# Softmax times values, bound by transfers: the load of the values moved to the end of a pass, and three small edits that go with it

## The chip, the cores and the metric

The kernel runs on one core of one Trainium2 chip. The metric is the device time of one execution, in microseconds (us). Executions of one kernel agree within about 0.15%. The time over the kernel before is always taken against its runs of the same rounds on the same chip. The 95% interval of such a ratio is 0.13 to 0.18% (1.4 to 1.9 us) to either side, so smaller differences between times settle nothing by themselves; each kernel has one trace. In lines of the profile, PE and PEld are TensorE's products and weight loads, DVE is VectorE, ACT ScalarE, POOL GpSimd, SP SyncE; a q marks an engine's sequencer, and L255 is line 255 of the kernel.

## The reference

```python
def reference(scores, v):          # scores (8, 12, 1024, 1024), v (8, 12, 1024, 64), float32
    scores_max = np.max(scores, axis=-1, keepdims=True)
    attn = np.exp(scores - scores_max)
    attn = attn / (np.sum(attn, axis=-1, keepdims=True) + 1e-8)
    return np.matmul(attn, v).astype(np.float32)
```

There are 96 heads. The scores are 403 MB, the values 25 MB, and 25 MB are written. The profile counts 436 MB read.

## The kernel before

One pass of the loop does four heads. A head's scores (4 MB) lie in one of four buffers. ScalarE takes the exp of two rows a partition at a time, TensorE transposes, VectorE copies, TensorE multiplies by the values and a column of ones, VectorE divides. The values of four heads come in one load of 1 MB; GpSimd casts them to 16 bits; VectorE spreads them. Outputs of two heads leave in one store of 128 rows of 4,096 bytes. SyncE issues every transfer, in program order, into one queue. The parts that matter:

```python
    def load_next(k, n0):                       # heads 0 and 1 of the next pass
        if k < AHEAD - 2:
            load(k, (n0 + (AHEAD + k)) % BH, cond=n0 < BH - AHEAD)

    def last(n0):                               # the end of a pass
        before = queued[-1:]
        with tc.If(n0 < BH - 2 * AHEAD) as cmp:             # an ordinary pass (22 of 24)
            queued[:] = before
            load(AHEAD - 2, (n0 + (2 * AHEAD - 2)) % BH)    # "third load"
            load_v((n0 + 2 * AHEAD) % BH)                   # the values
            load(AHEAD - 1, (n0 + (2 * AHEAD - 1)) % BH)    # "fourth load"
            store(n0, AHEAD - T)                            # "second store"
        with cmp.Else():
            with tc.If(n0 < BH - AHEAD) as cmp2:            # the penultimate pass
                queued[:] = before
                load(AHEAD - 2, BH - 2, (4, 4))
                load(AHEAD - 1, BH - 1, (4,))
                store(n0, AHEAD - T)
                load(AHEAD - 1, BH - 1, (2, 1, 1), 4)
            with cmp2.Else():                               # the last pass
                queued[:] = before
                store(n0, AHEAD - T)

    def heads(n0):
        for k in range(AHEAD):
            ...                                 # exp, transposes, copies, products
        while pending:
            finish(pending.pop(0))
        cast_v()
        last(n0)
```

The first store of a pass (heads 0 and 1) is issued while head 2 is worked on, ahead of the third load. So the queue of an ordinary pass is: load 0, load 1, first store, third load, values, fourth load, second store.

The softmax here doesn't subtract the row's maximum and nothing guards it: scores larger than these inputs give would overflow.

Of the kernel before, what the change touches and what calls it, by code (L numbers as in the profile page):

```python
# [8 lines left out]
FP32 = mybir.dt.float32  # L9
FP16 = mybir.dt.float16  # L10
EXP = mybir.ActivationFunctionType.Exp
# [3 lines left out]
def kernel(  # L15
# [6 lines left out]
    nc = tc.nc  # L22
    P = 128
# [4 lines left out]
    BH = B * H  # L28
# [7 lines left out]
    AHEAD = 4  # L36
# [11 lines left out]
    v_bh = v.rearrange("b h (i t) d -> (b h i) (t d)", i=Q)  # L48
# [6 lines left out]
    sb_pool = ctx.enter_context(tc.tile_pool(name="sbpool", bufs=1))  # L55
# [4 lines left out]
    order16 = const_pool.tile([P, P], FP16, name="order16")  # L60

    nc.vector.tensor_copy(  # L62
        out=order16[:].rearrange("p (t j) -> p t j", t=T),
        in_=ident32[:].rearrange("p (j t) -> p t j", t=T),
# [11 lines left out]
    def buffers(pool, count, shape, dtype, name):  # L76
        return [pool.tile(shape, dtype, name=f"{name}{k}") for k in range(count)]

    s_bufs = buffers(sb_pool, AHEAD, [P, R, SK], FP32, "s_nat")
    v_sb = sb_pool.tile([P, C // L, S, L, D], FP32, name="v_sb")  # L80
    v_half = sb_pool.tile([P, C // L, S, L, D], FP16, name="v_half")
    p_bufs = buffers(sb_pool, 8, [P, EB, SK], FP16, "p_nat")
    pt_bufs = buffers(sb_pool, 4, [P, SK], FP16, "pt")
    out_bufs = buffers(sb_pool, 2, [P, T, R, D], FP32, "out_sb")
# [8 lines left out]
    def take(bufs):  # L93
        k = turn.get(id(bufs), 0)
        turn[id(bufs)] = k + 1
        return bufs[k % len(bufs)]
# [4 lines left out]
    def after(a, b):  # L101

        tc.add_manual_dep(
            a.ins,
            b.ins.name,
            mybir.DependencyInfo(mybir.DependencyClass.NoSync, mybir.DependencyReason.DATA),
            reason="order",
        )

    def queue(dma):  # L110

        if queued:
            after(dma, queued[-1])
        queued.append(dma)

    def one(bh, n):
        return bh[bass.ds(n, 1)].rearrange("o p r d -> (o p) r d")

    def normalise(k, st, first, last):

        psO = psO_whole if k % 2 == 0 else psO_banks[first]
        psO = psO[:, :, 0 : G * M].rearrange("p b (g m) -> p b g m", m=M)
        recip = st["recip"][:, first:last]
        nc.vector.reciprocal(out=recip, in_=psO[:, :, :, D : D + 1])  # L124
        h = k % T
        for t in range(T):
            part = slice(t * W, (t + 1) * W)
            rows = st["out_sb"][h * W : (h + 1) * W, t, first * G : last * G, :]
            nc.vector.tensor_tensor(  # L129
                out=rows.rearrange("j (b g) d -> j b g d", g=G),  # L130
                in0=psO[part, :, :, 0:D],
                in1=recip[part].to_broadcast([W, last - first, G, D]),
                op=mybir.AluOpType.mult,
            )

    def finish(u):

        n0, k, r, pt, st = u
        b, g = r // G, r % G
        if r == 0:  # L140
            st["recip"] = take(rc_bufs)
            st["out_sb"] = out_bufs[k // T]
        bank = psO_whole[:, b] if k % 2 == 0 else psO_banks[b][:, 0]
        for c in range(C):
            nc.tensor.matmul(  # L145
                out=bank[:, g * M : (g + 1) * M],
                lhsT=pt[:, c * P : (c + 1) * P],
                rhs=st["vones"][:, c, 0:M],
                start=(c == 0),
                stop=(c == C - 1),  # L150
            )
        if k % 2 == 1:
            if g == G - 1:
                normalise(k, st, b, b + 1)
        elif r == R - 1:
            normalise(k, st, 0, R // G)
        if r == R - 1 and k == T - 1:
            store(n0, 0)

    def store(n0, k):  # L160

        rows = out_bh.rearrange("(m x) y -> m x y", x=P)
        dma = nc.sync.dma_start(
            out=rows[bass.ds((n0 + k) // T, 1)].rearrange("o x y -> (o x) y"),
            in_=out_bufs[k // T][:].rearrange("x t r d -> x (t r d)"),
        )
        for other in stores:
            apart(dma, other)
            apart(other, dma)
        apart(dma, dma)  # L170
        stores.append(dma)
        queue(dma)
# [3 lines left out]
    def apart(dma, other):  # L176
        tc.declare_no_dep(
            dma.ins, other.ins, across_iterations=True, reason="stores of two heads are disjoint"
        )

    def load(k, n, parts=(R,), r=0, **cond):
        for rows in parts:
            queue(
                nc.sync.dma_start(  # L184
                    out=s_bufs[k][:, r : r + rows, :],
                    in_=one(sc_bh, n)[:, r : r + rows, :],
                    **cond,
                )
            )
            r += rows  # L190

    def load_v(n):

        rows = v_bh.rearrange("(m x) y -> m x y", x=P)
        queue(
            nc.sync.dma_start(  # L196
                out=v_sb[:].rearrange("x h s l d -> x (h s l d)"),
                in_=rows[bass.ds(n // AHEAD, 1)].rearrange("o x y -> (o x) y"),
            )
        )  # L200

    def cast_v():
        nc.gpsimd.tensor_copy(out=v_half[:], in_=v_sb[:])  # L203

    def spread_v(k, s, behind=None):

        copy = nc.vector.tensor_copy(  # L207
            out=vones_bufs[k][s * Q : (s + 1) * Q, :, 0:D].rearrange(
                "i (h l) d -> i h l d", l=L
            ),  # L210
            in_=v_half[k * Q : (k + 1) * Q, :, s],
        )
        if behind is not None:
            after(copy, behind)

    def load_next(k, n0):

        if k < AHEAD - 2:
            load(k, (n0 + (AHEAD + k)) % BH, cond=n0 < BH - AHEAD)

    def last(n0):


        before = queued[-1:]

        with tc.If(n0 < BH - 2 * AHEAD) as cmp:  # L226
            queued[:] = before
            load(AHEAD - 2, (n0 + (2 * AHEAD - 2)) % BH)
            load_v((n0 + 2 * AHEAD) % BH)
            load(AHEAD - 1, (n0 + (2 * AHEAD - 1)) % BH)  # L230
            store(n0, AHEAD - T)
        with cmp.Else():
            with tc.If(n0 < BH - AHEAD) as cmp2:
                queued[:] = before
                load(AHEAD - 2, BH - 2, (4, 4))
                load(AHEAD - 1, BH - 1, (4,))
                store(n0, AHEAD - T)
                load(AHEAD - 1, BH - 1, (2, 1, 1), 4)
            with cmp2.Else():
                queued[:] = before  # L240
                store(n0, AHEAD - T)

    def heads(n0):

        for k in range(AHEAD):
            if k == 0:
                for s in range(S):
                    spread_v(k, s)
            st = dict(vones=vones_bufs[k])
            for r in range(R):  # L250
                if r % EB == 0:
                    p_nat = take(p_bufs)
                    rows = 1 if k == AHEAD - 1 and r == R - EB else EB
                    for g in range(0, EB, rows):
                        nc.scalar.activation(  # L255
                            out=p_nat[:, g : g + rows, :].rearrange(
                                "p r (x v) -> p x r v", v=Q * L
                            ),
                            in_=s_bufs[k][:, r + g : r + g + rows, :].rearrange(
                                "p r (i x l) -> p x (r i) l", i=Q, l=L  # L260
                            ),
                            func=EXP,
                        )
                p_row = p_nat[:, r % EB, :].rearrange("p (h q l) -> p h l q", q=P, l=L)
                psT = take(psT_bufs)
                for c in range(C):
                    nc.tensor.transpose(  # L267
                        out=psT[:, c * P : (c + 1) * P],
                        in_=p_row[:, c // L, c % L, :],
                        identity=order16[:],  # L270
                    )
                pt = take(pt_bufs)
                copy = nc.vector.tensor_copy(out=pt[:], in_=psT[:])  # L273
                if k < AHEAD - 1 and r % (R // S) == 0:
                    spread_v(k + 1, r // (R // S), copy)
                if r == R - 1:
                    load_next(k, n0)
                pending.append((n0, k, r, pt, st))
                if len(pending) > LAG:
                    finish(pending.pop(0))  # L280
        while pending:
            finish(pending.pop(0))
        cast_v()
        last(n0)

    assert BH % AHEAD == 0 and BH >= 2 * AHEAD and SK == Q * S * C
# [38 lines left out]
```

## Time and profile before

| | kernel before |
|---|---|
| time, median of the first 3 runs | 1065.68 us (1065.58 to 1066.06) |
| span of the profiled run | 1064.0 us |
| DMA queue | 453.00 MB, 99.2% of the time of 16 engines |
| busiest compute engine | DVE, 74% |
| one pass in the middle | 43.68 us |
| start of the last head's exps to the end | 18.0 us |

The pass is a fifth of the windows of five passes that the prediction shows. What bounds the kernel is read there too.

A landing in the trace is sixteen records, one for each DMA engine ("ring" below). In the kernel before, twelve rings land a score load within about 0.6 us of each other, three land 2 to 2.5 us after the median of these twelve, a lag that they get in the first 70 us and keep, and one ring, at first among the twelve, drifts: its lag over the fast rings grows from 0.4 us (at 69 us) to 2.3 us (at 1030 us).

### The profile page before, as it was taken

How to read it: one execution, taken by the hardware profiler on the slowest of the kernel's cores; microseconds unless marked ns; L12 is line 12 of the kernel's file. 1: busy time of each engine (PE TensorE's matmuls, PEld its weight loads, DVE VectorE, ACT ScalarE, POOL GpSimd, SP SyncE). 2: the span in 40 equal slices, each digit the busy share in tenths (PEclk: the TensorE clock that was granted, in tenths of full speed). 3: DMA queues.
4: the chain of work that ended last, by engine and by line, in shares of the span. 5: the costliest groups of instructions: out<-in, count | busy, mean ns of one | idle time of the engine just before them, and what ended most of it. 6: DMA issues, size and time to landing. Idle time of an engine off the chain costs nothing.

```text
span 1064.0 us, 32161 instructions
## 1 busy us (share of the span) xinstructions
PE 731.4 (69%) x12288; PEld 678.4 (64%) x12288; DVE 786.6 (74%) x1589; ACT 735.6 (69%) x432; POOL 48.1 (5%) x31
## 2 busy tenths in 40 slices
PE   2766766767766677677686776867666777666676
PEld 2665756667666667666575665767565666666675
DVE  3776876868768777677786776868768687687777
ACT  3766776666767668586676866667766668676685
POOL 0000000000000000000000000000000000000000
PEclk9888888878889888888988888888889788898989
DMA  9999999999999999999999999999999999999995
GB/s 397 431 418 434 426 433 434 433 434 432 432 434 432 425 443 430 429 431 428 433 431 436 432 434 434 431 434 424 441 427 434 432 426 435 432 432 428 440 425 236
DMA packets 24772, 453.06 MB, mean 426 GB/s; under 512 B 2752, under 2 KB 2752, under 8 KB 9152
## 3 DMA queue, kind: packets, MB, share of 16 engines
q1 hardware_dynamic: 24768, 453.00, 99.2%
q8 instruction: 4, 0.07, 0.0%
HBM read 436.21 MB, written 25.17 MB: 434 GB/s over the span
## 4 chain that ended last, share of the span: by engine, by line
DMA 81%; ACT 12%; issue 3%; ACTq 1%; PE 1%; DVE 0%; SPq 0%; PEld 0%; DVEq 0%
DMA s_nat<-in_scores_dram 81%; ACT p_nat L255 12%; PE psT L267 1%; ACTq L255 1%; ACTq L226 0%; ACTq L292 0%; PE psO L145 0%; DVE pt L273 0%; PE psO_whole L145 0%; SPq L184 0%; PEld L267 0%; ACTq L320 0%; DVE out_sb L129 0%; SPq L196 0%; PEld L145 0%
## 5 line engine op out<-in xcount | busy, mean ns | idle before, releaser
L255 ACT ACTIVATE p_nat<-s_nat 128x2048 f16<-128x2048 f32 (+1 forms) x408 | 704.8, 1799 | 228.1 <-DMA s_nat<-in_scores_dram 202.2
L267 PE MATMUL psT<-order,p_nat 128*128 128x128 f16 x6144 | 574.9, 246 | 269.9 <-ACT p_nat L255 263.9
L273 DVE COPY pt<-psT 128x1024 f16<-128x1024 f16 x768 | 515.8, 687 | 200.6 <-PE L267 109.4
L267 PEld LDWEIGHTS <-p_nat 128*128 128x128 f16 x6144 | 446.5, 123 | 298.3 <-ACT p_nat L255 295.7
L145 PEld LDWEIGHTS <-pt 128*128 128x128 f16 x6144 | 302.9, 107 | 81.0 <-DVE pt L273 77.7
L145 PE MATMUL psO<-vones,pt 128*128 128x65 f16 x3072 | 177.4, 201 | 53.9 <-DVE pt L273 50.2
L145 PE MATMUL psO_whole<-vones,pt 128*128 128x65 f16 x3072 | 189.9, 211 | 2.7 <-DVE pt L273 2.4
L207 DVE COPY vones<-v_half 32x512 f16<-32x512 f16 x384 | 109.4, 285 | 22.8 <-POOL v_half L203 6.0
L255 ACT ACT_TABLE_LOAD x24 | 30.8, 1283 | 89.8 <-DMA s_nat<-in_scores_dram 81.7
L203 POOL CAST v_half<-v_sb 128x2048 f16<-128x2048 f32 x25 | 47.4, 1896 | 1002.3 <-DVE vones L207 957.1
L129 DVE TENSOR_TENSOR out_sb<-psO,recip 64x256 f32<-64x256 f32 x192 | 81.1, 423 | 6.1
L129 DVE TENSOR_TENSOR out_sb<-psO_whole,recip 64x512 f32<-64x512 f32 x96 | 66.1, 688 | 3.0
L124 DVE RECIPROCAL recip<-psO 128x4 f32<-128x4 f32 x96 | 17.1, 178 | 34.4 <-PE psO L145 17.6
L124 DVE RECIPROCAL recip<-psO_whole 128x8 f32<-128x8 f32 x48 | 9.7, 203 | 4.5 <-PE psT L267 3.9
L71 DVE MEMSET vones<- 128x16 f16 x4 | 0.2, 72 | 0.8 <-PEq L309 0.8
L62 DVE CAST order<-ident 128x128 f16<-128x128 f32 x1 | 0.2, 227 | 0.4 <-POOL ident masks.py:199 0.4
masks.py:199 POOL TENSOR_SCALAR_AFFINE_SELECT ident<-ident 128x128 f32<-128x128 f32 x1 | 0.3, 295 | 0.1
masks.py:197 POOL MEMSET ident<- 128x128 f32 x1 | 0.2, 205 | 0.3 <-POOLq L309 0.3
L309 POOL MEMSET const-float32-0.0<- 128x1 f32 x1 | 0.1, 100 | 0.2 <-issue 0.2
L309 POOL MEMSET const-bfloat16-1.0<- 128x1 bf16 x1 | 0.1, 103 | 0.0
L309 POOL MEMSET const-uint8-127<- 128x1 uint8 x1 | 0.1, 103 | 0.0
L309 POOL MEMSET const-float32-1.0<- 128x1 f32 x1 | 0.1, 100 | 0.0
## 6 DMA issues: line engine op xcount, KB each, us to landing
s_nat<-in_scores_dram SPq DMA_DIRECT2D x96, 4096.0 KB, 35.8
v_sb<-in_v_dram SPq DMA_DIRECT2D x24, 1024.0 KB, 33.1
out_dram<-out_sb SPq DMA_DIRECT2D x48, 512.0 KB, 26.9
s_nat<-in_scores_dram SPq DMA_DIRECT2D x3, 2048.0 KB, 32.4
s_nat<-in_scores_dram SPq DMA_DIRECT2D x1, 1024.0 KB, 25.4
s_nat<-in_scores_dram SPq DMA_DIRECT2D x2, 512.0 KB
```

The source lines that it names most:

```text
L62: nc.vector.tensor_copy(out=order16[:].rearrange("p (t j) -> p t j", t=T), in_=ident32[:].rearrange("p (j t) -> p t j", t=T),)
L71: nc.vector.memset(vo[:, :, D : D + 2], 1.0)
L124: nc.vector.reciprocal(out=recip, in_=psO[:, :, :, D : D + 1])
L129: nc.vector.tensor_tensor(out=rows.rearrange("j (b g) d -> j b g d", g=G), in0=psO[part, :, :, 0:D], in1=recip[part].to_broadcast([W, last ...
L145: nc.tensor.matmul(out=bank[:, g * M : (g + 1) * M], lhsT=pt[:, c * P : (c + 1) * P], rhs=st["vones"][:, c, 0:M], start=(c == 0), stop=(c ...
L203: nc.gpsimd.tensor_copy(out=v_half[:], in_=v_sb[:])
L207: copy = nc.vector.tensor_copy(out=vones_bufs[k][s * Q : (s + 1) * Q, :, 0:D].rearrange("i (h l) d -> i h l d", l=L), in_=v_half[k * Q : ( ...
L255: nc.scalar.activation(out=p_nat[:, g : g + rows, :].rearrange("p r (x v) -> p x r v", v=Q * L), in_=s_bufs[k][:, r + g : r + g + rows, :] ...
L267: nc.tensor.transpose(out=psT[:, c * P : (c + 1) * P], in_=p_row[:, c // L, c % L, :], identity=order16[:],)
L273: copy = nc.vector.tensor_copy(out=pt[:], in_=psT[:])
L309: nc = _bacc.Bacc("TRN2", target_bir_lowering=False, num_devices=1)
```

## The change

Its intent: the values are not needed early, so they go behind the pass's last store, and the fourth score load comes up 1 MB of queue earlier. A transfer of 16 rows of 4 bytes fills the place of the values, so that both branches hand out the same completion semaphores to the loads that follow. A one-column exp at the head of the body makes ScalarE load its table there rather than after the wait for head 0's scores. The cast is written ahead of the last head.

```diff
     v_half = sb_pool.tile([P, C // L, S, L, D], FP16, name="v_half")
+    spare = sb_pool.tile([P, 1], FP16, name="spare")
+    short = sb_pool.tile([16, 1], FP32, name="short")
 ...
+    def align():
+        queue(nc.sync.dma_start(out=short[:], in_=v_bh[0:16, 0:1]))
 ...
             load(AHEAD - 2, (n0 + (2 * AHEAD - 2)) % BH)
-            load_v((n0 + 2 * AHEAD) % BH)
+            align()
             load(AHEAD - 1, (n0 + (2 * AHEAD - 1)) % BH)
             store(n0, AHEAD - T)
+            load_v((n0 + 2 * AHEAD) % BH)
 ...
                 store(n0, AHEAD - T)
+                align()
                 load(AHEAD - 1, BH - 1, (2, 1, 1), 4)
 ...
+        table = nc.scalar.activation(out=spare[:], in_=order16[:, 0:1], func=EXP)
         for k in range(AHEAD):
 ...
-                        nc.scalar.activation(
+                        exp = nc.scalar.activation(
 ...
+                        if k == r == g == 0:
+                            after(exp, table)
 ...
+            if k == AHEAD - 2:
+                cast_v()
         while pending:
             finish(pending.pop(0))
-        cast_v()
         last(n0)
```

## The prediction

> **What bounds the kernel now.** I read the page first: shares, slices, the chain, bytes.
>
> ```profile
> q1 hardware_dynamic: 24768, 453.00, 99.2%
> HBM read 436.21 MB, written 25.17 MB: 434 GB/s over the span
> ...
> DMA s_nat<-in_scores_dram 81%; ACT p_nat L255 12%; PE psT L267 1%; ACTq L255 1%; ACTq L226 0%; ACTq L292 0%; PE psO L145 0%; DVE pt L273 0%; PE psO_whole L145 0%; SPq L184 0%; PEld L267 0%; ACTq L320 0%; DVE out_sb L129 0%; SPq L196 0%; PEld L145 0%
> ```
>
> One queue's packets fill 99.2% of the time of sixteen DMA engines, while no compute engine is busy more than 74% (DVE). The chain is a score load, the exp that frees its buffer, the next load: this alone could be a latency loop (four buffers), which earlier exps would shorten. So I asked whether the transfer engines ever rest, with sums over windows of whole passes (a pass is four heads):
>
> ```profile
> 181.52:399.90 218.38, 153.80 (x2560) 142.98 (x2560) 163.88 (x330) 153.25 (x92) 9.48 (x5) 0.84 1.01 432
> 399.90:618.30 218.40, 154.13 (x2560) 143.39 (x2560) 163.88 (x330) 153.20 (x91) 9.48 (x5) 0.84 1.00 432
> 618.30:836.68 218.38, 153.14 (x2560) 142.21 (x2560) 163.86 (x330) 153.24 (x91) 9.48 (x5) 0.84 1.01 432
> ```
>
> The last two columns are the DMA share and GB/s: full in every group of five passes, 218.38/5 = 43.68 us a pass. The bytes agree: four loads of 4,096 KB, 1,024 KB of values and two stores of 512 KB are 18.87 MB, and 18.87 MB / 43.68 us = 432 GB/s. The loop is bound by transfer bandwidth. Next, how far the queue runs ahead: the issues of one pass in order of time.
>
> ```profile
> 437.00 0.36 SPq L163 DMA_DIRECT2D out_dram<-out_sb  x1
> 437.92 0.34 SPq L184 DMA_DIRECT2D s_nat<-in_scores_dram  x1
> 442.85 0.33 SPq L196 DMA_DIRECT2D v_sb<-in_v_dram  x1
> 449.34 0.33 SPq L184 DMA_DIRECT2D s_nat<-in_scores_dram  x1
> 456.05 0.36 SPq L163 DMA_DIRECT2D out_dram<-out_sb  x1
> 463.76 0.34 SPq L184 DMA_DIRECT2D s_nat<-in_scores_dram  x1
> ```
>
> A score load lands 35.8 us after its issue (median on the page), though 4.19 MB alone need 4.19/0.432 = 9.7 us: some 26 us are queue. The thinnest moment is before 463.76: the load issued at 449.34 lands at about 485.4, the store behind it 1.2 us later, so about 22.8 us of work are still queued then. ScalarE's side of the same stretch:
>
> ```profile
> 452.66 1.28 ACT L255 ACT_TABLE_LOAD   x1 [3.46 <-DMA s_nat<-in_scores_dram]
> 453.96 7.31 ACT L255 ACTIVATE p_nat<-s_nat 128x2048 f16<-128x2048 f32 x4
> 462.42 7.32 ACT L255 ACTIVATE p_nat<-s_nat 128x2048 f16<-128x2048 f32 x4 [1.16 <-SPq L226]
> 473.30 7.32 ACT L255 ACTIVATE p_nat<-s_nat 128x2048 f16<-128x2048 f32 x4 [3.55 <-DMA s_nat<-in_scores_dram]
> 485.48 1.91 ACT L255 ACTIVATE p_nat<-s_nat 128x2048 f16<-128x2048 f32 x1 [4.86 <-DMA s_nat<-in_scores_dram]
> ```
>
> Every head begins with idle time in brackets: ScalarE waits for data, the table load included. What is left is the tail, from the chain in order of time:
>
> ```profile
> 1013.46 32.39 DMA s_nat<-in_scores_dram
> ...
> 1045.96 1.92 ACT p_nat L255
> ...
> 1058.81 0.38 DVE out_sb L129
> ```
>
> The first half of the last head lands at 1045.86; exps, products and the last store take the remaining 18.1 us.
>
> **What the Trainium skill says.** "DMA: Bandwidth & Descriptors", section Specifications, gives a fabric ceiling of 435 GB/s, below which it puts an HBM limit of about 358 GB/s per core, and says that under 512 B a transfer becomes a read-modify-write. The 432 GB/s agree with the first figure and contradict the second; no data transfer below 4,096 B occurs before, so the third is untested and is my main doubt on the new 64 byte one. The same page, Queues, rings and completion order, has each engine consume its ring in order: the landing times agree (each issue lands after those before it), so bytes put earlier delay what follows, and reordering moves no total. "ScalarE: Activation LUTs", What ACT_TABLE_LOAD costs, gives about 1,283 ns plus 1,380 ns of drain: the page's row has 1,283 ns, but the exp starts 20 ns after the load here, so no drain shows. "GPSIMD Engine Reference", Specifications, says that GpSimd shares its SBUF interfaces with VectorE, which matters where the cast moves; at 48.33 us the cast ran beside a 0.69 us VectorE copy in 1.90 us, as alone.
>
> **The change part by part.**
> *Table load.* 23 passes after the first carry a 1,283 ns load after the wait for head 0. It moves before the wait; a one-column exp joins it. ScalarE then does head 0 about 1.28 us earlier and waits longer for head 1. The work saved on that path is 23 x 1.28 = 29.5 us, and none lies on the path that sets the end: the buffer freed earlier is refilled by a load queued behind more than 20 us of others. In the last pass the same: head 1's first exp waits 1.08 us for data at 1030.12 before, so that slack just grows to 2.4. In the first, the table load (8.06 us) is over long before data (15.31). Gain 0.
> *Values last.* In 22 passes 1.05 MB move from ahead of the fourth score load to behind the second store. 1.05/0.432 = 2.43 us: the fourth load lands and its exps start 2.4 us earlier, the first load of the next pass lands as before, the values land later. Issue near 456.5 and landing behind the fourth load (483.0) and the store (484.2) put them at about 487, 30 us after issue. The bytes ahead of any later load are the same. Gain 0. In the last two passes no values are loaded, so the tail's order is as it was.
> *Cast.* It waits for VectorE's last spread of head 3 (near 484 now) wherever it stands in the program; now the values (487) end its wait. It finishes near 489; head 0 of the next pass spreads at 500.2 before, some 2.4 us earlier after, so about 8 us spare.
> *The 64 byte transfer.* 23 of them. The trace's packet records give mean times of 159 ns for 4,096 B, 309 for 8,192 and 1,214 for 32,768: a line through them is about 8 ns per packet plus bytes at 27.2 GB/s, and the 4 byte semaphore writes last 9 ns. One 4 byte packet and one semaphore write on each ring are about 17 ns, and 23 x 17 ns = 0.4 us of DMA time, all on the bound. Its issue costs SyncE about 0.34 us, in a queue that is over 20 us ahead.
> *Semaphores.* The records name eight completion semaphores, given out in order. SyncE makes up, in each ordinary pass, for three transfers that only the penultimate branch has (66 semaphore writes at L226 = 22 x 3). Before, these sit on those of no transfer, load 0 and load 1; with the extra one they move to load 0, load 1 and the first store, which lands about 1.2 us after load 1 (462.3): the issue at 463.76 becomes about 464. In the penultimate pass the last row's load likewise waits for a store landing near 1031.5 instead of 1030.1, with some 18 us still queued. Cost 0.
> *Sum.* 1065.68 + 0.4, less nothing: 1066, rounded down a little to 1065.9, because 17 ns may overlap its neighbours.
>
> **Rivals.**
> *The ScalarE path is the real loop.* The chain has 12% ACT, and 1.28 us off each pass would make 29 us, so about 1036. Against it: the DMA share of 1.00 to 1.01 leaves nothing to fill; 434 bytes a ns would have to become 445. Rejected at nearly certainty.
> *Small transfers stall the rings.* If a read-modify-write with a serial memory round trip cost every ring 1 us, 23 us would come on: 1089. For: the 512 B warning. Against: the packets of different transfers follow each other without a gap (share 1.0 across all borders). At 0.1 us each it is 2.3 us, 1068.
> *A new wait dries the queue.* If SyncE had to wait for a transfer just issued, 30 us or more would be lost in each pass. For: the alignment exists because such waits do. Against: by the count above it waits only for transfers issued 20 us and more before. If a late cast or a wait for the first store held it a few us, the 22.8 us of queue would hide it: 1066.
> *Rings in step.* A landing waits for the slowest of sixteen rings; at the end four land 1.6 to 2.7 us after the other twelve, a lag that they keep from 62 to 65 us on, where some packets took 1.7 to 2.9 us instead of 1.21. A different order at the start could make that lag smaller or larger: minus 1.5 to plus 1 us.
>
> **Range and chances.** The three runs before span 0.5 us. To that come ring lag (1 to 1.5 us either way) and a small packet of up to 0.1 us (plus 2 us). Hence 1064.3 to 1067.6. Faster by 2% needs 21 us off a bandwidth bound with unchanged bytes: 0.5%. Slower by 2% needs a dry queue or a serial round trip: 1.5%.
>
> **What would show it.** Right: the sums over five passes again have a DMA share of 1.00 and 432 GB/s at 43.7 us a pass; the table load follows the previous pass's last exp, and head 0's exp starts at about 452.7 on this page's time, with longer waits for data elsewhere; head 3's exp starts 2.4 us earlier; GpSimd's waits change from VectorE's spread to the values' landing; values land about 30 us after issue. Wrong: a DMA share well under 1 in the loop, a pass other than 43.6 to 43.8 us, SyncE issuing head 0's load more than 10 us later, or VectorE waiting for the cast.

## The result, and the profile after

The changed kernel took 1069.38 us (median of 4 runs, 1068.60 to 1069.61), the kernel before 1065.87 us in 4 runs. That is 3.5 us slower. The ratio is 1.0031, with a 95% interval of 1.0013 to 1.0048. Ratios here are the mean time of one kernel's runs over that of the other's of the same rounds, so not quite the ratio of the medians. The predicted range, 1064.3 to 1067.6, missed it. The profiled run is the quickest of the four (1068.60 us, span 1066.6), so the trace shows 2.6 us of the loss.

First the page of the changed kernel, queue and bytes, and then its row of GB/s in 40 slices:

```profile
GB/s 397 431 425 433 418 445 431 433 433 425 435 429 433 429 430 431 430 433 431 433 433 433 429 436 433 431 433 431 434 433 433 426 438 433 433 433 431 434 423 199
...
q1 hardware_dynamic: 25504, 453.00, 99.0%
...
HBM read 436.21 MB, written 25.17 MB: 433 GB/s over the span
```

The same row of the kernel before:

```profile
GB/s 397 431 418 434 426 433 434 433 434 432 432 434 432 425 443 430 429 431 428 433 431 436 432 434 434 431 434 424 441 427 434 432 426 435 432 432 428 440 425 236
```

Same bytes, same rate almost everywhere. There are 736 packets more, 23 times 16 data packets and 16 semaphore writes. Only the last slice differs clearly: 199 for 236 GB/s. Now the windows of five passes each, early and late in the changed kernel. The columns are the window, its length, busy time of PE, PEld, DVE, ACT and POOL, clock, DMA share, GB/s:

```profile
190.49:408.96 218.47, 151.30 (x2560) 140.39 (x2560) 164.33 (x331) 154.32 (x95) 9.47 (x5) 0.85 1.01 432
803.81:1023.24 219.43, 152.59 (x2560) 141.99 (x2560) 164.13 (x330) 154.30 (x95) 9.47 (x5) 0.84 1.01 432
```

Both windows run from one pass's first exp to that of five passes on. The early one takes 218.47 us, which is the pace of the kernel before (218.38). The late one takes 219.43 us, 43.89 us a pass, 0.2 us more, and yet the DMA share is 1.01 and the rate 432 GB/s as before. Passes that get longer at full and equal throughput are the riddle: a mean over sixteen rings can stay full while the one ring that every landing waits for falls behind the other fifteen.

ScalarE in the middle of the changed kernel, in order of time:

```profile
446.66 1.28 ACT L255 ACT_TABLE_LOAD   x1
447.96 0.21 ACT L255 ACTIVATE spare<-order 128x1 f16<-128x1 f16 x1
452.65 7.32 ACT L266 ACTIVATE p_nat<-s_nat 128x2048 f16<-128x2048 f32 x4 [4.49 <-DMA s_nat<-in_scores_dram]
462.29 7.32 ACT L266 ACTIVATE p_nat<-s_nat 128x2048 f16<-128x2048 f32 x4 [2.32 <-SPq L233]
473.27 7.32 ACT L266 ACTIVATE p_nat<-s_nat 128x2048 f16<-128x2048 f32 x4 [3.66 <-DMA s_nat<-in_scores_dram]
```

The table load now follows the last exp of the pass before. Head 0 starts at 452.65 instead of 453.96, and head 1 at 462.29 against 462.42: the 1.3 us are gone into waiting for head 1, as foreseen.

The issues of the same pass:

```profile
436.55 0.36 SPq L165 DMA_DIRECT2D out_dram<-out_sb  x1
437.47 0.34 SPq L186 DMA_DIRECT2D s_nat<-in_scores_dram  x1
442.88 0.34 SPq L226 DMA_DIRECT2D short<-in_v_dram  x1
446.76 0.33 SPq L186 DMA_DIRECT2D s_nat<-in_scores_dram  x1
452.48 0.36 SPq L165 DMA_DIRECT2D out_dram<-out_sb  x1
453.17 0.33 SPq L198 DMA_DIRECT2D v_sb<-in_v_dram  x1
```

The fourth load is issued at 446.76 instead of 449.34, the second store at 452.48 instead of 456.05. The values go out at 453.17 and their cast starts at 486.80:

```profile
486.80 1.89 POOL L205 CAST v_half<-v_sb 128x2048 f16<-128x2048 f32 x1 [41.89 <-DVE pt L286]
```

The values have landed at 486.65, just before this start. The profile puts this wait down to a VectorE copy that ended at about the same time; of the 25 casts it puts the waits of 13 down to the landing of the values.

One wait is new. From SyncE's own list of waits (total us, times, longest):

```profile
SPq L226 <- DMA v_sb<-in_v_dram: 104.7, 21, 5.4
```

The 64 byte transfer of an ordinary pass waits until the values of the pass before have landed, because both branches write the same small tile on different semaphores. It ends at about 442.9, and the fourth load behind it isn't due before 446.7.

The tail, from the chain in order of time:

```profile
1013.57 35.21 DMA s_nat<-in_scores_dram
...
1048.89 1.92 ACT p_nat L266
...
1061.74 0.38 DVE out_sb L131
```

The last head's exps start at 1048.89 instead of 1045.96, 2.9 us later. From there to the end of the span it is 17.7 us, before 18.0. So the tail is the same and the loads land later.

The rings' landing records tell why. Lag is the time by which the last of sixteen rings lands load 1 after the median of the twelve fastest:

| landing of load 1 at about | 69 | 244 | 419 | 594 | 769 | 944 us |
|---|---|---|---|---|---|---|
| before: the drifting ring | 0.4 | 0.5 | 1.1 | 1.4 | 1.7 | 2.1 |
| before: the last ring | 2.6 | 2.5 | 2.5 | 2.5 | 2.5 | 2.5 |
| after: the drifting ring | 0.2 | 0.9 | 1.9 | 2.8 | 3.7 | 4.6 |
| after: the last ring | 2.4 | 2.4 | 2.4 | 2.8 | 3.7 | 4.6 |

(The drifting ring is told from the three steady ones by its changing lag; records don't name rings.) Before, the drifting ring stays hidden behind three rings that are 2.5 us late anyway. After, it drifts twice as fast, comes out from behind them near 500 us, and from then on every score load is as late as this ring. That the semaphore counts sixteen engines that finish on their own is what the Trainium skill says in "DMA: Bandwidth & Descriptors", Why a DMA increments its semaphore by 16 and not by 1; the trace agrees, with landings of one transfer spread over up to 5.5 us in the changed kernel.

The last score load of all lands 3.0 us later than before (1055.05 against 1052.05). The twelve fast rings land it 0.25 us later (median 1049.81 against 1049.56), about what the small transfers add (0.23 us, see below); the other 2.75 us are the growth of the last ring's lag, from 2.49 to 5.24 us.

Where does this ring lose the time? Its lag steps up at the stores. The packet records say the same. A store's 4,096 byte packet takes 159 ns; between 100 and 1040 us, 88 of them took more than 160.5 ns before, and 202 after, mostly 173 to 192 ns. They belong to the drifting ring: of the 51 slow packets of the changed kernel after 800 us, every one ran when the other fifteen rings were through with that store. What they took beyond 159 ns sums to 1.6 us before and 4.3 us after; the difference, 2.8 us, agrees with the 2.75 us of added lag.

Most of the difference comes from the second store, the one behind which the values now stand. At the first store of a pass 68 slow packets became 93, at the second 20 became 109. In the changed kernel each store has four to six of them; in the kernel before the second store has none after 400 us. e18 below has 87 and 104.

The 32,768 byte packets of the loads kept their mean, 1,214.4 ns in both.

### The profile page after: what moved, and what is told of

It is laid out like the page before. It is cut to its first block, busy times and chain, and to the rows that moved or that the text cites. A ratio compares the mean times of both kernels' runs of the same rounds, so it can differ in the third digit from the quotient of the medians.

```text
span 1066.6 us, 32260 instructions
## 1 busy us (share of the span) xinstructions
PE 726.3 (68%) x12288; PEld 673.9 (63%) x12288; DVE 788.5 (74%) x1589; ACT 740.8 (69%) x456; POOL 48.0 (5%) x31
## 5 line engine op out<-in xcount | busy, mean ns | idle before, releaser
L147 PEld LDWEIGHTS <-pt 128*128 128x128 f16 x6144 | 296.4, 106 | 84.4 <-DVE pt L286 81.9
L147 PE MATMUL psO_whole<-vones,pt 128*128 128x65 f16 x3072 | 184.3, 208 | 2.4 <-DVE pt L286 2.3
L255 ACT ACT_TABLE_LOAD x24 | 30.8, 1283 | 1.9 <-ACTq L306 1.5
L255 ACT ACTIVATE spare<-order 128x1 f16<-128x1 f16 x24 | 4.9, 206 | 0.3
```

The source lines that it names most:

```text
L147: nc.tensor.matmul(out=bank[:, g * M : (g + 1) * M], lhsT=pt[:, c * P : (c + 1) * P], rhs=st["vones"][:, c, 0:M], start=(c == 0), stop=(c ...
L255: table = nc.scalar.activation(out=spare[:], in_=order16[:, 0:1], func=EXP)
```

## The experiments

Each ran five times (e18 six) beside the kernel before, all correct. "Slow packets" are counted as above. "Fast" and "last" ring are the mean time of a pass, over 20 passes, by the landings of load 1 on the median of the twelve fastest rings and on the last of all sixteen. The runs came on four chips; the slow ring is on each: e1, e5, e9 and e13, on chips 13, 0, 9 and 7, time as the kernel before and have 87, 89, 75 and 87 slow packets. So it is not one faulty chip.

| run | values | extra transfer | time | over before | fast ring | last ring | slow packets |
|---|---|---|---|---|---|---|---|
| kernel before | ahead of fourth load | none | | | 43.676 | 43.674 | 88 |
| the change | last | ahead of fourth load | 1069.38 | +3.5 | 43.686 | 43.809 | 202 |
| e1 tiles only | as before | none | 1065.93 | +0.1 | 43.676 | 43.674 | 87 |
| e2 tiles declared last | last | ahead of fourth | 1069.23 | +3.4 | 43.688 | 43.814 | 195 |
| e3 table only | as before | none | 1065.81 | 0.0 | 43.675 | 43.674 | 85 |
| e4 no early exp | last | ahead of fourth | 1069.18 | +3.4 | 43.686 | 43.837 | 198 |
| e5 extra only | as before | behind second store | 1065.85 | 0.0 | 43.687 | 43.686 | 89 |
| e6 last, halves | last | none | 1066.47 | +0.6 | 43.720 | 43.718 | 11 |
| e7 ahead of second store | between fourth load and store | ahead of fourth | 1067.62 | +1.8 | 43.686 | 43.746 | 143 |
| e8 wide extra | last | ahead of fourth, 512 B rows | 1069.40 | +3.5 | 43.704 | 43.838 | 201 |
| e9 cast only | as before | none | 1065.90 | 0.0 | 43.675 | 43.674 | 75 |
| e10 cast at end | last | ahead of fourth | 1068.74 | +2.9 | 43.686 | 43.812 | 200 |
| e11 halves only | as before | none | 1067.89 | +2.0 | 43.722 | 43.718 | 13 |
| e12 last, unaligned | last | none | 1066.74 | +0.9 | 43.676 | 43.674 | 42 |
| e13 extra there | as before | ahead of fourth | 1066.03 | +0.3 | 43.687 | 43.686 | 87 |
| e14 extra later | last | behind fourth | 1067.34 | +1.6 | 43.687 | 43.686 | 40 |
| e15 change, halves | last | ahead of fourth | 1143.79 | +78.0 | 47.192 | 47.196 | 9 |
| e16 two tiles | last | ahead of fourth, no wait | 1069.33 | +3.2 | 43.686 | 43.823 | 192 |
| e17 extra first | last | ahead of third load | 1071.96 | +5.8 | 43.688 | 43.816 | 195 |
| e18 last, in time | last | none | 1072.35 | +6.3 | 43.676 | 43.783 | 191 |

Two columns carry the argument. The fast ring's pass moves only with the packets that a variant adds: 0.010 us for the 64 byte transfer, 0.045 us for halves. The last ring's pass moves away from the fast one's in just those variants that have some 140 slow packets or more.

### First call: address, table, or order

**e1_tiles_only.** The two tiles move the stores' source by 64 bytes in each partition.

```diff
+    spare = sb_pool.tile([P, 1], FP16, name="spare")       # kernel before, nothing else
+    short = sb_pool.tile([16, 1], FP32, name="short")
```

> The kernel before with only the two small tiles declared (never used), so that everything allocated after them, the source tiles of the stores among them, sits 64 bytes further on in each partition. In the trace of the changed kernel one of the sixteen rings falls about 0.25 us a pass further behind the fast ones (0.1 us a pass in the kernel before), stepping up at each store, and after some 14 passes it is the last to land. Theory A, the address: the stores' 4,096 byte rows no longer start on a 256 byte boundary, and this makes the slow ring slower: 1068.5 to 1069.8 us, 2.5 to 4 us over the kernel before, with the ring's lag near 5 us at the end. Theory B, the order of the transfers and the extra one: no change, within 0.5 us of before. Theory C, the early table load: no change.

Measured 1065.93 us against 1065.81, 87 slow packets. The address theory, which I held, falls. (The built program has its store tiles 64 bytes further on, though it drops the two tiles themselves as unused.)

**e2_tiles_last.**

```diff
-    spare = ... ; short = ...          # the change, the two tiles declared
     rc_bufs = buffers(...)
+    spare = ... ; short = ...          # behind all others
```

> The whole change, with the two small tiles declared behind all others, so that no address of the kernel before moves. Theory A: the loss goes, 1065.6 to 1066.6 us, at most 0.7 us over the kernel before (about 0.3 us of that for the 64 byte transfers), the slow ring's lag near 2.5 us at the end as before. Theories B and C: the loss stays, 1068.5 to 1069.8 us.

1069.23 us, 195 slow packets: the loss stays with the old addresses. Both runs say the same.

**e3_table_only.**

```diff
+        table = nc.scalar.activation(out=spare[:], in_=order16[:, 0:1], func=EXP)   # kernel before
```

> The kernel before with only the one-column exp at the head of the loop body, its tile declared last. Theories A and B: within 0.4 us of the kernel before, with the table load right behind the last exp of the pass before. Theory C, the earlier exps set something moving that costs time: 1067.5 us or more.

1065.81 us against 1065.81. The early table load costs nothing and gains nothing, as the prediction has it.

**e4_order_only.**

```diff
-        table = nc.scalar.activation(out=spare[:], ...)     # the change without it; tile last
```

> The changed kernel without the one-column exp and with the 64 byte tile declared last: values last, the 64 byte transfer, the cast moved. Theory A: 1065.6 to 1066.6 us. Theory B, the values behind the second store or the extra transfer make the slow ring fall behind: 1068.5 to 1069.8 us, a lag near 5 us at the end. Theory C: as the kernel before.

1069.18 us, and 5.2 us of lag at 989 us. Order or the extra transfer (or the cast, which was still in it) remain.

### Second call: order or extra transfer

**e5_extra_only.**

```diff
             store(n0, AHEAD - T)
+            align()                    # kernel before; likewise in the penultimate pass
```

> The kernel before (values still ahead of the fourth score load, cast at the end) with only the 64 byte transfer added behind the second store. Two theories are left after the first four runs. Order: the values straight behind the second store make the store packets of one ring slow. Small transfer: its 4 byte packets do. By order: 1065.8 to 1066.4 us, the slow ring's lag near 2.4 us at the end as before, some 90 slow packets among the stores' 4,096 byte ones. By small transfer: 1068.5 to 1069.8 us, a lag near 5 us, some 200 slow packets.

1065.85 us against 1065.87, 89 slow packets: a small transfer by itself costs 0.011 us a pass on every ring and no time that the runs resolve.

**e6_last_halves.**

```diff
-            load(AHEAD - 2, ...)
-            load_v(...)
+            load(AHEAD - 2, ..., (4, 4))
             load(AHEAD - 1, ...)
             store(n0, AHEAD - T)
+            load_v(...)
```

> The kernel before with the values last, and no small transfer: the third score load goes in two halves instead, which gives the same semaphores. The halves double the packets of that load, 8 more of some 8 ns on each ring and pass, so 1.5 us in 22 passes by themselves. By order: 1070 to 1071.5 us with the slow ring's lag near 5 us at the end. By small transfer: 1066.9 to 1067.8 us, a lag near 2.5 us.

1066.47 us, outside both forecasts, and only 11 slow packets. The halves cost 0.044 us a pass on every ring, not the 0.07 us that I had reckoned. At this point it looked as if values last were harmless without the small transfer. That was a wrong turn: e11 shows that halves calm the slow ring whatever the order is.

**e7_before_store.**

```diff
             load(AHEAD - 1, ...)
-            store(n0, AHEAD - T)
             load_v(...)
+            store(n0, AHEAD - T)       # the change; penultimate pass: align() ahead of its store
```

> The whole change, but with the values between the fourth score load and the second store, so that the second store is again followed by a score load. By order: the steps of the lag at the second store go, so the time falls to 1065.9 to 1067.3 us. By small transfer: 1068.5 to 1069.8 us as in the change.

1067.62 us, between the two: 143 slow packets, a last ring at 43.746 us a pass. Half the step back in order gives half the loss.

**e8_wide_extra.**

```diff
-    short = sb_pool.tile([16, 1], FP32)      ... in_=v_bh[0:16, 0:1]
+    short = sb_pool.tile([16, 128], FP32)    ... in_=v_bh[0:16, 0:128]
```

> The whole change with the extra transfer widened from 16 rows of 4 bytes to 16 rows of 512 bytes, the size from which the Trainium skill sees no read-modify-write. By order: as the change, 1068.5 to 1070 us. By small transfer, if its size is what hurts: 1065.9 to 1067 us; if an extra transfer of any size hurts: as the change.

1069.40 us, as the change. Rows of 512 bytes instead of 4 make no difference to the loss, so it doesn't come from rows under 512 bytes.

### Third call: cast, halves, and values last alone

**e9_cast_only** (the cast moved in the kernel before) and **e10_cast_at_end** (left at the end in the change):

```diff
+            if k == AHEAD - 2:
+                cast_v()
         while pending: ...
-        cast_v()                       # e9: this edit on the kernel before; e10: its reverse on the change
```

> The kernel before with only the cast moved ahead of the last head. So far the loss came in exactly those variants that have the cast moved AND the values last AND the extra transfer; it did not come from the extra alone, nor from values last with the third load in halves. Theory cast: the move makes the loss, 1068.5 to 1069.8 us. Theory position (values last needs to be there): as the kernel before within 0.4 us, a cast at the same time as before, some 90 slow store packets.

> The whole change with the cast left at the end of the loop body. Theory cast: 1065.8 to 1066.5 us, a lag near 2.4 us at the end. Theory position: as the change, 1068.5 to 1069.8 us, about 200 slow store packets, a lag near 5 us.

1065.90 us and 1068.74 us, with 75 and 200 slow packets. The place of the cast in the program does nothing.

**e11_halves_only.**

```diff
-            load(AHEAD - 2, (n0 + (2 * AHEAD - 2)) % BH)          # kernel before
+            load(AHEAD - 2, (n0 + (2 * AHEAD - 2)) % BH, (4, 4))
```

> The kernel before with only the third score load in two halves, values in their old place: the control for the run with values last and halves, which had hardly any slow store packets (11) and the slow ring never falling behind. If the halves calm that ring by themselves: few slow packets (under 30), and 1066.0 to 1066.8 us, the 0.6 to 1 us over the kernel before being the halves' own packets. If not: some 90 slow packets, 1066 to 1067.5 us; then it is the absence of the extra transfer that made the earlier run good.

13 slow packets, and the drifting ring is gone: the halves calm it by themselves. The time, 1067.89 us, is over the first forecast: the last load lands 0.9 us later, which the packets explain, and another 0.9 us are lost behind it in the tail. There ScalarE waits 2.40 us for TensorE before the last head's exps (1.14 us for data in the kernel before); why, I didn't follow up.

**e12_last_unaligned.**

```diff
             load(AHEAD - 2, ...)
-            align()                    # the change, no align() in either branch, cast at the end
             load(AHEAD - 1, ...)
             store(n0, AHEAD - T)
             load_v(...)
```

> The change reduced to the values behind the second store: no extra transfer, cast at the end, no one-column exp, so that the semaphores of the two branches no longer agree. Theory position alone (values last makes the store packets slow, and halves hid it): 1068.3 to 1069.8 us, about 200 slow packets. Theory interaction (values last and the extra transfer ahead of the fourth load are both needed) or theory cast: 1065.6 to 1066.3 us, under 110 slow packets. A wait that misaligned semaphores add would show as SyncE issuing a score load more than 10 us late and a DMA share under 0.98.

1066.74 us, 42 slow packets, last ring at 43.674. (My file still had the one-column exp, against what the expectation says; e3 shows that it does nothing.) The slow packets spoke for the interaction, the time lies 0.4 us over its range. But the issues differ too, as this kernel's timeline shows:

```profile
436.35 0.36 SPq L165 DMA_DIRECT2D out_dram<-out_sb  x1
442.87 7.64 SPq L186 DMA_DIRECT2D s_nat<-in_scores_dram  x2
457.61 0.35 SPq L165 DMA_DIRECT2D out_dram<-out_sb  x1
```

The third load goes out at 442.87 instead of 437.47, probably because one half of it in the penultimate branch now has the semaphore of the ordinary fourth load, and the fourth follows at 450.2 (442.87 + 7.64 less one issue). So this run changes two things, and I took it for one. All its slow packets are at the first store, none at the second: with the loads this late, values last did not make the second store slow.

### Fourth to sixth call

**e13_extra_there.**

```diff
             load(AHEAD - 2, ...)
+            load_v(...)                # the change with the values back in their place
             align()
             load(AHEAD - 1, ...)
             store(n0, AHEAD - T)
-            load_v(...)
```

> The change with the values back ahead of the fourth score load: third load, values, 64 byte transfer, fourth load, second store. If the extra transfer ahead of the fourth load is enough to make one ring's store packets slow, wherever the values stand: 1068.3 to 1069.8 us, some 200 slow packets. If both are needed: 1065.6 to 1066.5 us, under 110 slow packets.

1066.03 us, 87 slow packets. With the values in their old place the change loses nothing to speak of, though tile, early exp, cast and small transfer are all in.

**e14_extra_later.**

```diff
-            align()
             load(AHEAD - 1, ...)
+            align()                    # the change
             store(n0, AHEAD - T)
```

> The change with the extra transfer behind the fourth score load instead of ahead of it (third load, fourth load, extra, second store, values). Its semaphores do not agree between the branches, as in the run with values last and no extra, whose tail cost about 1 us. If values last plus an extra transfer anywhere in the pass is the cause: some 200 slow packets and 1069 to 1071 us. If only the place ahead of the fourth load does it: under 110 slow packets and 1066.3 to 1067.5 us.

1067.34 us, 40 slow packets, all at the first store. Again the third and fourth load are issued late (443.31 and 450.6), so it has the fault of e12.

**e15_change_halves.** Meant to take the slow packets out of the change by the halves.

```diff
-            load(AHEAD - 2, ...)
+            load(AHEAD - 2, ..., (4, 4))      # the change; align() moved to fit in the other branch
             align()
```

> The change with the third score load in two halves, which kept the store packets quick in the two runs that had it. If the slow store packets are the cause of the loss, and the halves take them away here too: under 40 slow packets, the slow ring no further than 2.5 us behind at the end, and 1066.3 to 1068.2 us although 8 packets are added on each ring and pass. If the loss comes from something else that goes with the change: 1069.5 us or more, 3.5 us for the change and up to 1.5 us for the halves.

1143.79 us, for a reason that I hadn't meant. With one transfer more in the pass, the values got the semaphore of load 0. SyncE's waits:

```profile
SPq L186 <- DMA v_sb<-in_v_dram: 481.0, 22, 22.1
```

Now load 0 can't be issued until the values, which are the last thing in the queue, have landed: 22 us in each of 22 passes. The queue runs dry, and from 400 to 1000 us the profile has a DMA share of 0.96 and 400 GB/s. It says nothing on the slow packets, but it shows the kind of wait that the 64 byte transfer was meant to prevent, and what the prediction's third rival looks like when it comes true. (Leaving the small transfer out, in e12 and e18, brought no such wait.)

**e16_two_tiles.**

```diff
+    short2 = sb_pool.tile([16, 1], FP32, name="short2")
 ...
-                align()                # penultimate branch of the change
+                align(short2)
```

> The whole change, with a tile of its own for the extra transfer of the penultimate branch. In the change both branches write one tile, so that SyncE holds the extra transfer, and the fourth load behind it, until the values of the pass before have landed (104.7 us of waiting in all at that line); here this wait is gone, and every transfer is the same. If the wait has to do with the slow store packets: under 120 of them, and 1065.8 to 1067 us. If only what stands in the queue counts: as the change, 1068.5 to 1069.8 us, some 200 slow packets, a lag near 5 us at the end.

1069.33 us, 192 slow packets, and the wait at that line is gone from the list. The new wait of the change is hidden and harmless.

**e17_extra_first.**

```diff
+            align()
             load(AHEAD - 2, ...)
-            align()                    # e16 otherwise
```

> As the run before it in this call, with the extra transfer ahead of the third score load instead of behind it; values last as in the change. If the place between third and fourth load is needed: under 120 slow packets, 1065.8 to 1067 us. If values last plus an extra transfer anywhere ahead of the fourth load does it, and no wait is needed: some 200 slow packets, 1068.5 to 1069.8 us.

195 slow packets, last ring at 43.816: as the change. The time is 1071.96 us, 2.6 us over e16, while the last load lands no later (1055.2 us, 1055.5 in e16); the rest is lost in the tail. The trace shows the place: the last head but one waits 3.76 us, until 1044.20, for its load to be whole, as in e18 below, while in e16 its exps start on the first half. Probably the semaphores of the halves no longer agree there; no run tests that.

**e18_last_timely.** Values last, no small transfer, and the third load in time.

```diff
             load(AHEAD - 2, ...)
-            load_v(...)                # kernel before
             load(AHEAD - 1, ...)
             store(n0, AHEAD - T)
+            load_v(...)
 ...
-                load(AHEAD - 2, BH - 2, (4, 4))
+                load(AHEAD - 2, BH - 2)          # penultimate pass only
```

> The kernel before with the values last and no extra transfer, no early exp, cast at the end; in the penultimate pass alone the third load goes whole, so that the third load of the ordinary passes no longer waits for the fourth load of the pass before (in the earlier run without the extra transfer it did, and was issued 5 us later than in the change; that run also still had the early exp, against what its expectation says). The whole load in the penultimate pass costs the tail 1 to 3 us by itself. If the extra transfer is needed for the slow store packets: under 110 of them, the slow ring no more than 2.6 us behind at the end, 1066.5 to 1069 us. If values last with the third load issued in time is enough, and the calm of the earlier run came from its late issue: about 200 slow packets, a lag near 5 us, 1069.5 to 1072.5 us.

191 slow packets, last ring at 43.783 us a pass against 43.676 of the fast ones, a lag of 5.3 us at the end. So moving the values behind the second store, with the loads in time, is enough; the small transfer isn't needed. One thing came with it unmeant, a wait of the fourth load for the values of the pass before:

```profile
SPq L184 <- DMA v_sb<-in_v_dram: 101.3, 21, 5.1
```

It doesn't delay that load (issued at 447.1, in e16, which has no such wait, at 446.87), and e16 shows that the loss needs no wait. But no run with whole loads issued in time has neither the wait nor the small transfer. Of the 6.3 us, 2.8 are the later landing of the last load (1054.84 against 1052.05 us). The rest, 3.5 us, is the tail, put down to the whole load in the penultimate pass; 1 to 3 us were expected of that. ScalarE there:

```profile
1032.75 7.32 ACT L255 ACTIVATE p_nat<-s_nat 128x2048 f16<-128x2048 f32 x4 [1.04 <-DMA s_nat<-in_scores_dram]
1043.86 14.63 ACT L255 ACTIVATE p_nat<-s_nat 128x2048 f16<-128x2048 f32 x9 [3.80 <-DMA s_nat<-in_scores_dram]
```

The last head but one must wait 3.80 us for its load to be whole; in the kernel before it followed without a pause (eight exps from 1030.12 on). The timed median is 1072.35 us.

No experiment beat the kernel before; e1, e3, e5 and e9 equal it.

## Why the prediction was wrong, point by point

- **What bounds the kernel.** Right as far as it went: a transfer-bound loop with over 20 us of queue, in which ScalarE's savings buy nothing. It failed in taking sixteen rings for one pipe. The path that sets the end runs through the last ring, and the share of 1.00, which I read as leaving "nothing to fill", is a mean over all. Of the signs that I had named for being wrong, one came: late passes take 43.89 us, outside 43.6 to 43.8, with the share still at 1.01.
- **Table load, gain 0.** Right: e3 measured 0.0 us.
- **Values last, gain 0.** This step failed. It said: "The bytes ahead of any later load are the same. Gain 0." The bytes are the same, but not the time of the packets: with the values behind the second store, store packets of one ring take 173 to 192 ns instead of 159 ns about twice as often, at the second store above all, and the last landing slips by 0.11 to 0.12 us a pass (43.783 against 43.676 for the fast rings in e18, 43.809 against 43.686 in the change). The last load lands 3.0 us later in the change (1055.05 against 1052.05), 2.8 in e18. That is the loss of the traced run.
- **Cast.** Right: it starts at 486.80, predicted about 487, when the values have landed. These took 33.5 us from issue (predicted 30), because the issue came at 453.17 rather than 456.5: I had not carried the earlier fourth head through to the second store. Harmless.
- **The 64 byte transfer.** Right that it is cheap: 0.010 us a pass on the fast rings, 0.23 us in 23 passes, where I had 0.4; e5 and e13 measure 0.0 and 0.3 us in all.
- **Semaphores.** The cost of 0 was right. The account was incomplete: I foresaw the wait for the first store (load 0 at about 464; it went out at 464.83), and missed that the small transfer waits for the values of the pass before. e16 takes that wait away and saves nothing.
- **Rivals.** ScalarE as the loop: no. Small transfers stalling the rings: no (e5, e8). A new wait that dries the queue: not in the change, though e15 shows it at 78 us. **Rings in step** was the right rival, with the wrong cause and size. I wrote "minus 1.5 to plus 1 us" for a chance offset at the start; it is a drift that grows in every pass and comes to about 3 us. The prediction has four rings keep their lag from 62 to 65 us on; three do, and the fourth had drifted there from 0.4 us, which it misread. Having noted in the records that landings wait for the slowest ring, I should have followed each ring's lag through the passes: the drift of 0.1 us a pass was there before the change, and near the end (1030 us) 0.15 us short of showing.

**What stays open.** Why one ring's store packets are slow, and why the order matters to it, the records don't show: they carry no ring, no address and no reason. Halving the third load (e6, e11) takes them away in either order, and where the third and fourth load are issued late (e12, e14) a fifth of them is left. So it isn't the order alone but something that order, packet sizes and issue times together decide. e15 was to test that calming this ring rescues the change, and failed for another reason, so that link rests on the sums (2.8 us of excess packet time, 2.75 us of added lag at the last load, 2.9 us later exps) and on the table, in which last ring and slow packets go together in all twenty kernels. Of the 3.5 us between the medians, 2.6 are in the trace, whose run was the quickest of its four; the untraced runs can't be split, but e2, the change with its two tiles placed elsewhere, was traced at 1069.57 us, and there the last load lands 3.3 us later than before. The smaller losses of e11, e12, e14 and e17 behind the last landing weren't explored.

## What to carry to other kernels

In a kernel bound by transfers, do not stop at the mean share of the DMA engines: look at how far apart the engines land one transfer, and whether that distance grows from pass to pass, because every consumer waits for the last. Reordering transfers with the same bytes can change the pace of one engine by a few tenths of a per cent, so an order that already runs well is worth something, and a forecast of "no change" for a new order should leave room for that. Where branches of a loop issue different numbers of transfers, check which semaphore each gets: in one variant here a single transfer more made a load wait for the newest one in the queue and cost 7%.

## What the Trainium skill lacked or had wrong

- "DMA: Bandwidth & Descriptors", Specifications: the table gives about 358 GB/s of HBM bandwidth per core without saying there that this is the share with both cores of a pair busy, as the page does further down. So the prediction's "contradict" goes too far: 432 GB/s were read and written here by one core for a millisecond, near the page's fabric ceiling of 435.
- The same page, Latency and other measured facts, says that two of the sixteen engines are usually slower, with a guess at a cause, but has no word on a lag that adds up over a kernel: here one of sixteen fell 2 to 5 us behind in 22 passes, through store packets of 4,096 bytes at 173 to 192 ns instead of 159, and the place of a transfer in the queue changed how fast. Which engine it was the records don't say.
- The same page, Specifications, warns of read-modify-write under 512 B: a transfer of 16 rows of 4 bytes cost each ring about 0.010 us, one of 512 byte rows 0.028 us (fast ring's pass in e8, 43.704, less 43.676), so nothing of the kind showed for so small a transfer in a full queue.
- "ScalarE: Activation LUTs", What ACT_TABLE_LOAD costs: the 1,283 ns are right, the drain of about 1,380 ns didn't show, neither behind the load (an exp starts 20 ns after its end) nor, in the change, ahead of it (it starts at once after the exp before). The page gives the drain for a switch to another set; here exp's table is loaded again in each pass, which it doesn't speak of.
